# Two-layer attention kernel: paired probability-times-value matmuls and a zero-padded sink matmul

## The chip, the cores and the metric

The kernel runs on one core of one Trainium2 chip. The metric is the device time of one execution in microseconds; the time shown for a kernel is the median of its runs. A core has five engines that run their own instruction queues in order and meet at semaphores: TensorE (PE in the profile; its weight loads are the rows PEld), VectorE (DVE), ScalarE (ACT), GpSimd (POOL) and SyncE (SP), which issues most of the DMA loads.

## The reference

The reference computes three blocks over 512 latent tokens and 256 context tokens of 1024 features: an attention block with a window and a sink, a gated-scan block, and a second block with another attention, a state-space branch and routed experts. What matters here is the attention of the first block, for 16 heads in 4 groups that share keys and values:

```python
def softmax_with_sink(s, sink):
    sk = sink.astype(jnp.float32)[None, :, :, None, None]
    m = jnp.maximum(jnp.max(s, axis=-1, keepdims=True), sk)
    e = jnp.exp(s - m)
    return e / (jnp.sum(e, axis=-1, keepdims=True) + jnp.exp(sk - m))
...
    def attend_block(args):
        q, k, v, blk = args
        ...
        s_lat = jnp.einsum('bqhgd,bkhd->bhgqk', q, k).astype(jnp.float32)
        s_lat = jnp.where(ok, s_lat, NEG_INF)
        s_ctx = jnp.einsum('bqhgd,bkhd->bhgqk', q, k_ctx).astype(jnp.float32)
        p = softmax_with_sink(jnp.concatenate([s_lat, s_ctx], axis=-1), sink_g).astype(v.dtype)
        return (jnp.einsum('bhgqk,bkhd->bqhgd', p[..., :n_loc], v)
                + jnp.einsum('bhgqk,bkhd->bqhgd', p[..., n_loc:], v_ctx))
```

A block of 128 latent queries sees the blocks of keys to its left and right, itself, and the 256 context keys; a block of context queries sees the context keys alone. The sink is one more logit for each head that has no value. The second block's attention is causal, over 8 heads of 64 features, with a table of relative biases and no sink.

## The kernel before

**Scores.** The first attention is written in `layer0_attn`. `scores(qb, j)` works for one block of 128 queries and one group of four heads. For each head it fills a score tile `S` of two PSUM banks (`bank2`, a ring of two tiles): matmuls of the query with the high and the low part of the keys (L576, L577 for the window, L582, L583 for the context), two additions of a triangular mask (L579, L581), and the sink as one more column: a matmul of `one3`, three rows of ones, with `sink3`, the sink in three bf16 parts on three rows (L584). VectorE takes the maximum (L585), ScalarE the exponential with its sum (L593), VectorE the reciprocal (L595), and GpSimd multiplies the probabilities with it (L596).

**Values.** `values(*two)` works for two groups at once, because the output of a group has 64 features and so takes a half of the array's columns. For each tile of 128 keys, a chunk, it turns the probabilities of each group's four heads with four transposes (L617) into a bank `T`, copies the bank to SBUF (ScalarE for the first group, L623; VectorE for the second, L621), and issues one value matmul for each group (L626). Both write into one bank `O`, the first on partitions 0 to 63, the second on 64 to 127. Each matmul waits for the copy of its own group's operand.

**Numbers.** There are 12 rounds, 8 over latent and 4 over context queries. Latent blocks have 4 or 5 chunks, context blocks 2, for two pairs of groups each: 44 chunks, so 44 pairs of value matmuls. There are 96 heads by blocks, and so 96 score tiles and 96 sink matmuls.

**What stands around it.** The generators of scores and values are stepped in turn, so that the values of one round are issued between the scores of the next. Among them stand twelve calls of `mod_half`, which load weights of the modulation (the tiles `raw`) and multiply with them (L348). The banks of `bank()` are a ring of four, which `T`, `O` and the modulation share.

**Order.** The kernel's instructions are put in order by a scheduler that is part of the compiler: it simulates the engines as it goes and gives each engine's queue the order in which the simulated instructions became ready. The order is then fixed; the engines do not reorder on the chip. An added dependency so changes the order of the queues around it.

**The second attention** is in `block2_mix` and has the same pattern: `values` for two heads, with four chunks of 512, 384, 256 and 128 columns, transposes at L1551, copies at L1555 (ScalarE) and L1553 (VectorE), and value matmuls at L1557; 16 pairs. Beside them stand the projections of the gates (L240, L242, L244).

Of the kernel before, what the change touches and what calls it, by code (L numbers as in the profile page):

```python
# [12 lines left out]
BF = mybir.dt.bfloat16  # L13
# [47 lines left out]
class Small:  # L61
    """One packed array of per-partition columns."""
# [85 lines left out]
class Kern:  # L148
# [30 lines left out]
    def opened(self, pool):  # L179
        """(pool, stack that closes it)"""  # L180
        st = ExitStack()
        return st.enter_context(pool), st

    def scratch(self, side="right"):
        """Opens the pool of the norms' temporaries."""
        st = ExitStack()
        self.s = st.enter_context(self.tc.tile_pool(name="scratch", bufs=1, side=side))
        return st

    def residual(self, ctx):  # L190
        """Tiles of [lat0..3, ctx0, ctx1], the ctx ones in a pool of their own."""
# [17 lines left out]
    def unit(self, ap, r=None, to=None, after=None, pool=False):  # L209
        """The parts of 2048 columns of weights; after: what ACT and DVE are to do first."""  # L210
# [18 lines left out]
    def mm3(self, out, ah, al, bh, bl, start, stop):  # L229
        """out += (ah+al)^T (bh+bl) less the al bl term's 2^-24."""  # L230
# [5 lines left out]
    def mm3s(self, outs, ah, al, bhs, bls, start, stop):  # L236
        """Several moving operands over one stationary one."""
# [7 lines left out]

    def rsqrt(self, ss, n, dim):
        """1/sqrt(ss/dim + eps), [P, n]."""
# [20 lines left out]
    def prenorm(self, x, scale, shift, h, col, wide=True, dv=0, pool=False):  # L268
        """x [P tokens, D] -> columns col.. of h^T (hi, lo [P, KC, T])."""
# [28 lines left out]
    def postnorm(self, x, y, gate, pool=True):  # L298
        """x += y/rms(y) * gate; y is [P, D] as one AP or two."""
# [34 lines left out]
    def mod_half(self, pool, l, m, half, tag="rows", raws=("raw", "raw"), own=None):  # L334
        """Columns 512 half.. of modulation vector m of layer l."""
# [27 lines left out]
    def mod_affine(self, l, which, ks=slice(0, KC)):  # L363
        """Per-feature scale and shift of the pre-norm: for lat (0) and ctx (1)."""
# [13 lines left out]
    def mod_gate(self, l, which, b, pool):  # L378
        """gate * g_post on all partitions, [P, D]."""
# [13 lines left out]
    def inproj(self, hs, unit, m, outs, kcs=KC):  # L393
        """outs[g] [P features, N tokens] = (unit column chunk m)^T h^T of token group g."""
# [7 lines left out]
    def natproj(self, h, t, units, outs, kcs=KC):  # L402
        """outs [P tokens of tile t, 256] = h unit, for each unit; h's low part comes last."""
# [11 lines left out]
    def natproj1(self, h, t, unit, out, kcs=KC):  # L415
        """out [P tokens of tile t, 256] = h unit."""
# [11 lines left out]
def first_norm(K, h):  # L428
    """Modulations 0 and 1 of layer 0 and its first pre-norm, from the inputs."""
# [3 lines left out]
    with K.left("start") as sp, K.scratch():  # L433
# [23 lines left out]
        # the first half of the features goes ahead of the second half's modulations  # L457
# [15 lines left out]
def layer0_attn(K):  # L473
    """Attention of both streams: o^T of ctx and of lat (f32 [P, KC, T]), in a pool left open on the right."""
# [10 lines left out]
    with ExitStack() as left:  # L485
# [11 lines left out]
        # sink in three bf16 parts, one to a partition  # L497
        sk = qp.tile([P, 3, 16], BF, name="sk")
        sr = qp.tile([P, 16], F32, name="sr")
        sink3 = qp.tile([3, 16], BF, name="sink3")  # L500
        one3 = qp.tile([3, P], BF, name="one3")
        nc.vector.memset(one3, 1.0)
# [53 lines left out]
        with K.right("att", 2) as ap:  # L556
            def scores(qb, j):
                """exp(scores - max) of the group's four heads and 1 / their sums."""
# [42 lines left out]
            def values(*two):  # L601
                """The outputs of two groups, which take a half of the array's columns each."""
# [3 lines left out]
                for c, kt in enumerate(tiles):  # L606
# [7 lines left out]
                    for i, (_, _, pr, _, _) in enumerate(two):  # L614
# [5 lines left out]
                        if i:  # L620
                            nc.vector.tensor_copy(ts[i], T)  # L621
                        else:
                            nc.scalar.copy(ts[i], T)  # L623
                    for i, t in enumerate(ts):
                        vs = slice((j + i) * 64, (j + i) * 64 + 64)
                        nc.tensor.matmul(O[i * 64:i * 64 + 64], V[:, kt, vs], t, start=c == 0, stop=c == nt - 1,  # L626
                                         skip_group_check=True)
# [31 lines left out]
def out_full(K, w_units, tiles, finish, side="right", pre=(), cut=KC - 1, loaded=None, halves=False):  # L659
    """Tokens by D products of a whole [1024, D] matrix with o^T (f32), tile by tile: finish(i, [bank, bank])."""  # L660
    nc = K.nc
    with K.tc.tile_pool(name="wres", bufs=1, side=K.sides[side]) as wp:
# [20 lines left out]
        for x, (i, _, _) in enumerate(tiles):  # L683
            oh, ol = now
            bs = [K.bank(), K.bank()]
            if halves and x == len(tiles) - 1:
                # the last tile's first half comes early
# [20 lines left out]
def mlp(K, l, hs, nts, finish, swap, side, split=False, filler=None):  # L708
    """relu^2 MLP over token groups hs; swap() comes after the last use of hs; finish(i, [ap, ap]) gets
# [1374 lines left out]
```

## Time and profile before

| What | Value |
|---|---|
| median of 3 runs | 2373.97 us |
| lowest and highest | 2368.01 and 2375.52 us |
| span of the profiled execution | 2364.2 us |
| TensorE busy | 95% of the span |
| VectorE, ScalarE, GpSimd busy | 55%, 41%, 12% |
| mean granted clock of TensorE | 0.973 |

The profile is of one execution. Its span runs from its first to its last instruction; the time of that same execution is not given beside it, and the runs' median lies 9.8 us above the span, which holds what comes before the first and after the last instruction. "Busy" is the time in which an engine had an instruction in work. Matmuls are pipelined: a matmul's own duration is longer than the distance to the next one's start, and what a matmul occupies is read from the starts. The granted clock is given as a share of full speed: 1.00 is 2.4 GHz and 0.50 is 1.2 GHz.

### The profile page before, as it was taken

The numbers are of one execution on the slowest core, as the hardware profiler recorded it, in microseconds if no ns is written. First come the engines' busy times: TensorE is split into PE (matmuls) and PEld (weight loads), VectorE is DVE, ScalarE is ACT, GpSimd is POOL, SyncE is SP. The second block draws the span as 40 slices with busy tenths as digits, with TensorE's granted clock in tenths as the row PEclk, the third lists the DMA queues.
The fourth block names the chain that finished last, engine by engine and source line by source line (L and its number), as shares of the span: only waits on it lengthen the run. The fifth ranks groups of instructions, "written<-read, shape, count | busy, mean of one in ns | idle before, by whom it ended". The sixth has DMA issues, their size and how long they took to land. (4 is left out here: it accounts for less than half of the span.)

```text
span 2364.2 us, 31188 instructions
## 1 busy us (share of the span) xinstructions
PE 2247.1 (95%) x12608; PEld 1807.7 (76%) x12608; DVE 1306.8 (55%) x2201; ACT 969.3 (41%) x1515; POOL 291.6 (12%) x301
## 2 busy tenths in 40 slices
PE   7999999999999999989999999999999998797996
PEld 5865556888888888889977787788789875586875
DVE  3754445435444544551584558755555855347985
ACT  5434444641122112362454542222344444435874
POOL 0024431200000000230000100000030000012332
PEclk9989999999999999989999999999999999897998
DMA  6223333111121112112244223432323333567993
GB/s 280 72 90 108 107 131 120 36 54 56 69 72 54 66 60 72 36 52 72 92 180 160 84 72 108 141 107 94 109 96 99 134 121 100 147 240 278 322 310 106
DMA packets 53746, 278.10 MB, mean 118 GB/s; under 512 B 8864, under 2 KB 13360, under 8 KB 25184
## 3 DMA queue, kind: packets, MB, share of 16 engines
q1 hardware_dynamic: 42080, 248.75, 29.9%
q0 software_dynamic: 10704, 25.68, 3.8%
q8 instruction: 100, 1.64, 0.3%
q10 hardware_dynamic: 816, 1.66, 0.2%
q14 instruction: 46, 0.38, 0.1%
HBM read 263.49 MB, written 24.08 MB: 122 GB/s over the span
## 5 line engine op out<-in xcount | busy, mean ns | idle before, releaser
L213 ACT CAST whi<-raw 128x2048 fp32r<-128x2048 f32 x106 | 202.5, 1910 | 538.1 <-PE b L244 365.7
L214 DVE TENSOR_TENSOR wlo<-raw,whi 128x2048 fp32r<-128x2048 f32 x106 | 245.3, 2315 | 279.0 <-ACT whi L213 273.1
L240 PE MATMUL b<-hl,whi 128*128 128x512 f32 (+1 forms) x736 | 283.1, 385 | 1.7 <-ACT whi L213 1.7
L242 PE MATMUL b<-hl,whi 128*128 128x512 f32 (+1 forms) x736 | 283.7, 386 | 0.6 <-DVE hl L296 0.6
L783 DVE TENSOR_TENSOR acc<-acc,b 128x512 f32<-128x512 f32 x280 | 180.7, 683 | 185.3 <-PE b L244 185.3
L244 PE MATMUL b<-hl,wlo 128*128 128x512 f32 (+1 forms) x736 | 281.8, 387 | 0.0
L240 PE MATMUL b<-whi,hid 128*128 128x512 f32 x640 | 215.8, 396 | 1.8 <-DVE acc L783 1.8
L242 PE MATMUL b<-wlo,hid 128*128 128x512 f32 x640 | 217.2, 395 | 0.1
L244 PE MATMUL b<-whi,hid 128*128 128x512 f32 x640 | 214.5, 396 | 0.0
L240 PEld LDWEIGHTS b<-hl,whi 128*128 128x128 f32 x736 | 139.1, 189 | 31.3 <-ACT whi L213 2.5
L244 PEld LDWEIGHTS b<-hl,wlo 128*128 128x128 f32 x736 | 139.0, 189 | 29.5 <-issue 1.2
L242 PEld LDWEIGHTS b<-hl,whi 128*128 128x128 f32 x736 | 139.1, 189 | 29.1 <-issue 1.8
L1940 DVE TENSOR_TENSOR wlo<-raw,whi 128x2048 fp32r<-128x2048 f32 x57 | 130.0, 2289 | 29.2 <-ACT whi L1940 29.2
L242 PEld LDWEIGHTS b<-wlo,hid 128*128 128x128 f32 x640 | 120.5, 189 | 28.3 <-DVE wlo L214 0.5
L244 PEld LDWEIGHTS b<-whi,hid 128*128 128x128 f32 x640 | 120.7, 189 | 28.0
L240 PEld LDWEIGHTS b<-whi,hid 128*128 128x128 f32 x640 | 119.8, 189 | 28.5 <-DVE acc L783 2.2
L596 POOL TENSOR_TENSOR p<-p,t 128x512 f32<-128x512 f32 (+2 forms) x96 | 91.9, 968 | 234.7 <-DVE t L595 138.3
L1940 ACT CAST whi<-raw 128x2048 fp32r<-128x2048 f32 x57 | 108.3, 1911 | 10.5 <-PE b L234 10.5
L232 PE MATMUL b<-whi,hl 128*128 128x256 f32 x320 | 91.3, 285 | 2.3 <-ACT qr L1448 2.3
L233 PE MATMUL b<-wlo,hl 128*128 128x256 f32 x320 | 91.5, 286 | 0.0
L234 PE MATMUL b<-whi,hl 128*128 128x256 f32 x320 | 91.1, 285 | 0.0
L585 DVE TENSOR_REDUCE t<-b 128x1 f32<-128x513 f32 (+2 forms) x96 | 61.4, 644 | 52.1 <-PE b L584 50.9
(607 smaller groups left out, 4780.2 us busy)
## 6 DMA issues: line engine op xcount, KB each, us to landing
raw<-in_w_e_dram SPq DMA_DIRECT2D x57, 1024.0 KB, 7.2
raw<-in_w_mod_dram SPq DMA_DIRECT2D x48, 1024.0 KB, 5.0
raw<-in_w_mlp_in_dram SPq DMA_DIRECT2D x32, 1024.0 KB, 4.8
raw<-in_w_mlp_out_dram SPq DMA_DIRECT2D x32, 1024.0 KB, 4.8
raw<-in_w_in_dram SPq DMA_DIRECT2D x16, 1024.0 KB, 4.9
raw<-in_gla_in_dram SPq DMA_DIRECT2D x12, 1024.0 KB, 4.8
raw<-in_w_o_dram SPq DMA_DIRECT2D x8, 1024.0 KB, 5.0
raw<-in_w_qkv_dram SPq DMA_DIRECT2D x6, 1024.0 KB, 10.8
```

The costliest lines, as they stand in the source:

```text
L213: ins = self.nc.scalar.copy(hi, r).ins
L214: ins = ins, (self.nc.gpsimd if pool else self.nc.vector).tensor_sub(lo, r, hi.bitcast(F32)).ins
L232: mm(out, ah, bh, start=start, stop=False)
L233: mm(out, ah, bl, start=False, stop=False)
L234: mm(out, al, bh, start=False, stop=stop)
L240: mm(o, ah, b, start=start, stop=False)
L242: mm(o, ah, b, start=False, stop=False)
L244: mm(o, al, b, start=False, stop=stop)
L585: nc.vector.reduce_max(nmx[:, g:g + 1], S[:, a0:a0 + n], axis=AX.X, negate=True)
L596: nc.gpsimd.tensor_mul(p[:, :n - 1], p[:, :n - 1], den[:, g:g + 1].to_broadcast([P, n - 1]))
L783: nc.vector.tensor_add(a, a, bs[n])
L1940: ins = K.nc.scalar.copy(hi, r).ins, K.nc.vector.tensor_sub(lo, r, hi.bitcast(F32)).ins
```

## The change

The value matmuls keep their operands. A new function adds a dependency: the first matmul of a pair also waits for the copy that was issued last, which is the second group's operand on VectorE. Since both operands are then there for both matmuls, the scheduler finds them ready together. The sink's two operands get 128 partitions in place of three, with zeros in 125 of them. (The changed file also has its comments and descriptions blanked, and so line numbers move by 6 to 8: L617 is now L625, L621 and L623 are L628, L626 is L632, L584 is L592, L1551 is L1558, L1557 is L1562.)

```diff
+    def together(self, two, copied):
+        self.tc.add_manual_dep(two[0], copied.name, mybir.DependencyInfo(mybir.DependencyClass.Sync,
+                                                                         mybir.DependencyReason.DATA),
+                               reason="side by side")
...
-        sink3 = qp.tile([3, 16], BF, name="sink3")
-        one3 = qp.tile([3, P], BF, name="one3")
-        nc.vector.memset(one3, 1.0)
+        sink3 = qp.tile([P, 16], BF, name="sink3")
+        one3 = qp.tile([P, P], BF, name="one3")
+        nc.vector.memset(sink3, 0.0)
+        nc.vector.memset(one3, 0.0)
+        nc.vector.memset(one3[0:3], 1.0)
...
-                        if i:
-                            nc.vector.tensor_copy(ts[i], T)
-                        else:
-                            nc.scalar.copy(ts[i], T)
+                        copied = (nc.vector.tensor_copy if i else nc.scalar.copy)(ts[i], T).ins
+                    both = []
                     for i, t in enumerate(ts):
                         vs = slice((j + i) * 64, (j + i) * 64 + 64)
-                        nc.tensor.matmul(O[i * 64:i * 64 + 64], V[:, kt, vs], t, start=c == 0, stop=c == nt - 1,
-                                         skip_group_check=True)
+                        both.append(nc.tensor.matmul(O[i * 64:i * 64 + 64], V[:, kt, vs], t, start=c == 0,
+                                                     stop=c == nt - 1, skip_group_check=True).ins)
+                    K.together(both, copied)
...
-                        if i:
-                            v.tensor_copy(pt[:, i, d], T[:, d])
-                        else:
-                            nc.scalar.copy(pt[:, i, d], T[:, d])
+                        copied = (v.tensor_copy if i else nc.scalar.copy)(pt[:, i, d], T[:, d]).ins
+                    both = []
                     for i, (h, _, _) in enumerate(two):
-                        nc.tensor.matmul(O[64 * i:64 * i + 64, d], V[:, kt, h * 64:h * 64 + 64], pt[:, i, d],
-                                         start=kt == 0, stop=kt == 3, skip_group_check=True)
+                        both.append(nc.tensor.matmul(O[64 * i:64 * i + 64, d], V[:, kt, h * 64:h * 64 + 64],
+                                                     pt[:, i, d], start=kt == 0, stop=kt == 3,
+                                                     skip_group_check=True).ins)
+                    K.together(both, copied)
```

TensorE's queue in the first attention, kernel before, at the end of a pair of groups with five chunks. `pt` tiles hold the copied operands of two chunks, `b_2091` and `b_2126` are banks `T`, `p` are probabilities and `b_1917` is `O`:

```order
L617 MATMUL b_2091<-ident,p_1859 128x128
L617 MATMUL b_2091<-ident,p_1872 128x128
L617 MATMUL b_2091<-ident,p_1885 128x128
L617 MATMUL b_2091<-ident,p_1898 128x128
L626 MATMUL b_1917<-pt_2014,v 64x512
L617 MATMUL b_2126<-ident,p_265_1904 128x128 x3
L617 MATMUL b_2126<-ident,p_2010 128x128
L626 MATMUL b_1917<-pt_2084,v 64x512
```

The two value matmuls of a chunk stand apart, with transposes between them.

The same engine and the same groups, changed kernel (`b_1919` is `O` here; the pair of `pt_2016` has its second operand from a bank whose transposes stand just ahead of the first row shown):

```order
L632 MATMUL b_1919<-pt_1920,v 64x512 x2
L625 MATMUL b_2046<-ident,p_236_1739 128x128 x3
L625 MATMUL b_2046<-ident,p_1846 128x128
L625 MATMUL b_2052<-ident,p_1861 128x128
L625 MATMUL b_2052<-ident,p_1874 128x128
L625 MATMUL b_2052<-ident,p_1887 128x128
L625 MATMUL b_2052<-ident,p_1900 128x128
L590 MATMUL b_302_2117<-KH_428,Q_418 128x256
L591 MATMUL b_302_2117<-KL_432,Q_418 128x256
L592 LDWEIGHTS one_446
L592 MATMUL b_302_2117<-sink_445,one_446 128x1
L632 MATMUL b_1919<-pt_2016,v 64x512 x2
```

Each pair stands together (x2), and between two pairs stand the transposes of the next chunk and a score.

TensorE's queue in the second attention, last pair of heads, kernel before (`b_15346` and `b_15345` are the banks `T` of the second and the first head):

```order
L1551 MATMUL b_15346<-ident,p_16253 128x128
L1551 MATMUL b_15346<-ident,p_16294 128x128
L1551 MATMUL b_15346<-ident,p_16311 128x128
L1551 MATMUL b_15346<-ident,p_16346 128x128
L1557 MATMUL b_2356_15342<-pt_16367,v_13895 64x512
L1551 MATMUL b_15346<-ident,p_16294 128x128
L1551 MATMUL b_15346<-ident,p_16311 128x128
L1551 MATMUL b_15346<-ident,p_16346 128x128
L1557 MATMUL b_2356_15342<-pt_16380,v_13895 64x384
L1551 MATMUL b_15345<-ident,p_16220 128x128
L1557 MATMUL b_2356_15342<-pt_16380,v_13895 64x384
```

The same place, changed kernel:

```order
L1558 MATMUL b_15348<-ident,p_16255 128x128
L1558 MATMUL b_15348<-ident,p_16296 128x128
L1558 MATMUL b_15348<-ident,p_16313 128x128
L1558 MATMUL b_15348<-ident,p_16348 128x128
L1562 MATMUL b_2356_15344<-pt_16369,v_13897 64x512 x2
L1558 MATMUL b_15348<-ident,p_16296 128x128
L1558 MATMUL b_15348<-ident,p_16313 128x128
L1558 MATMUL b_15348<-ident,p_16348 128x128
L1558 MATMUL b_15347<-ident,p_16222 128x128
L1562 MATMUL b_2356_15344<-pt_16382,v_13897 64x384 x2
L1558 MATMUL b_15348<-ident,p_16313 128x128
L1558 MATMUL b_15348<-ident,p_16348 128x128
```

The first of each pair has moved down to the second, behind the second operand's transposes.

## Rows read from the trace of the kernel before

**Rows 1.** Page, first part: busy time, share of the span and instructions of each engine

```profile
PE 2247.1 (95%) x12608; PEld 1807.7 (76%) x12608; DVE 1306.8 (55%) x2201; ACT 969.3 (41%) x1515; POOL 291.6 (12%) x301
```

**Rows 2.** Windows: stretch, length, busy time of each engine, granted clock, DMA share, GB/s

```profile
130.00:392.00 262.00, 257.23 (x1568) 145.21 (x1567) 131.01 (x302) 112.20 (x260) 91.91 (x96) 0.97 0.32 112
...
1880.00:1995.00 115.00, 110.20 (x484) 75.11 (x483) 66.26 (x192) 54.54 (x113) 7.06 (x16) 0.97 0.28 96
```

**Rows 3.** TensorE's waits, 130 to 392 us: total, times, longest

```profile
PE b L576 <- ACT p L593: 1.8, 2, 1.3
```

**Rows 4.** Timeline, TensorE, first attention: start, duration, instruction, count

```profile
228.57 1.08 PE L626 MATMUL b<-pt,v 128*64 128x512 f32 x4
229.58 0.66 PE L617 MATMUL b<-ident,p 128*128 128x128 f32 x4
230.17 1.07 PE L626 MATMUL b<-pt,v 128*64 128x512 f32 x2
231.17 0.66 PE L617 MATMUL b<-ident,p 128*128 128x128 f32 x4
231.59 0.42 PE L576 MATMUL b<-KH,Q 128*128 128x384 f32 x1
...
386.24 1.93 PE L626 MATMUL b<-pt,v 128*64 128x512 f32 x6
```

**Rows 5.** Groups by line: shape, count, busy us, mean ns, idle before

```profile
L584 PE MATMUL b<-sink,one 3*128 3x1 bf16 x96 | 16.6, 173 | 0.0
```

**Rows 6.** Timeline, one score and its sink, matmuls and weight loads

```profile
211.36 0.34 PE L577 MATMUL b<-KL,Q 128*128 128x384 f32 x1
...
211.54 0.10 PEld L579 LDWEIGHTS <-identb 128*128 128x128 bf16 x1 [0.16 <-issue]
...
211.61 0.19 PEld L582 LDWEIGHTS b<-KH,Q 128*128 128x128 f32 x1
...
211.84 0.28 PE L583 MATMUL b<-KL,Q 128*128 128x256 f32 x1
...
212.04 0.09 PEld L584 LDWEIGHTS <-one 3*128 3x128 bf16 x1
...
212.15 0.14 PEld L617 LDWEIGHTS b<-ident,p 128*128 128x128 f32 x1
```

**Rows 7.** Timeline, TensorE, second attention, a 256-column matmul and its successor

```profile
1898.21 0.28 PE L1526 MATMUL b<-KL,Q 128*128 128x256 f32 x1
1898.33 0.39 PE L240 MATMUL b<-hl,whi 128*128 128x512 f32 x1
```

**Rows 8.** Timeline, TensorE: a sink, and the start of the score two later

```profile
210.98 0.17 PE L584 MATMUL b<-sink,one 3*128 3x1 bf16 x1
...
213.05 0.44 PE L576 MATMUL b<-KH,Q 128*128 128x384 f32 x1 [0.57 <-ACT p L593]
```

**Rows 9.** Lines L621 and L585, VectorE: ns min/median/max, first and last start

```profile
L621 DVE COPY pt<-b x44: 675/691/693, 164.2 to 385.7; 128x512 f32<-128x512 f32 x44
...
L585 DVE TENSOR_REDUCE t<-b x96: 408/692/827, 142.3 to 380.1; 128x1 f32<-128x513 f32 x32, 128x1 f32<-128x257 f32 x32, 128x1 f32<-128x641 f32 x32
```

**Rows 10.** Timeline, TensorE and VectorE, second attention, last pair of heads

```profile
1982.51 0.60 PE L1551 MATMUL b<-ident,p 128*128 128x128 f32 x4
1983.89 1.07 PE L1557 MATMUL b<-pt,v 128*64 128x512 f32 x2 [0.78 <-DVE pt L1553]
...
1983.15 0.69 DVE L1553 COPY pt<-b 128x512 f32<-128x512 f32 x1 [0.43 <-PE b L1551]
```

**Rows 11.** Page, DMA issues: count, KB each, median us to landing

```profile
raw<-in_w_e_dram SPq DMA_DIRECT2D x57, 1024.0 KB, 7.2
```

**Rows 12.** Windows at the start of the first attention, columns as in rows 2

```profile
145.00:148.00 3.00, 2.20 (x11) 1.73 (x11) 1.33 (x6) 2.97 (x6) 1.39 (x2) 0.80 1.03 431
148.00:151.00 3.00, 2.89 (x13) 2.11 (x13) 2.64 (x4) 1.56 (x4) 0.69 (x1) 0.50 0.26 107
```

**Rows 13.** Timeline, TensorE, the first value matmul of the stage

```profile
157.88 1.97 PE L626 MATMUL b<-pt,v 128*64 128x512 f32 x2
```

## The prediction

> **What bounds the kernel now.** The page's first part names TensorE: it works in 95% of the span [rows 1]. That is an average, so I cut the span at the two places that the change touches. From 130 to 392 us, the first layer's attention, TensorE is busy 257.23 of 262 us, VectorE 131.01, ScalarE 112.20 and GpSimd 91.91 [rows 2]. The longest reason among TensorE's waits of that stretch is 1.8 us in two times [rows 3]. So in this stage a microsecond that leaves TensorE's queue leaves the time, until another chain becomes the limit. In the second block's attention, 1880 to 1995 us, it is busy 110.20 of 115 us [rows 2], with its gaps near the end. After both stages comes work that is again TensorE's, and the loads of the expert weights are issued only as buffers come free, so an earlier start is kept.
>
> **The value matmuls of the first attention.** There are 44 pairs, 88 matmuls of 128x512, each recorded as two instructions (so x2 in the timeline is one matmul, x4 two). Each fills half of the array's columns. The timeline shows what a pair costs. Where both stand next to each other (x4) they take 228.57 to 229.58, 1.01 us; where one stands alone (x2) it takes 230.17 to 231.17, 1.00 us [rows 4]. The second half of the columns is free of charge if its matmul is next in the queue. Going through the timeline of the whole stage I count 61 entries of x2, 12 of x4 and one of x6 that lasts two units (the last row of the group): 75 units of 1.0 us. The new order has all 44 pairs adjacent, so 44 units. 31 units go, 31 us. Each unit that goes also takes its way in with it: four transposes lead to a value matmul after 0.59 us (229.58 to 230.17), while four transposes cost 0.42 where a score's matmul follows (231.17 to 231.59, [rows 4]): 0.17 us. After a sink matmul the way in costs the same as for any other work, so I take 0.1 on average, 3 us. Sum: -34 us; the ends are -31 and -36.
>
> By the Trainium skill (TensorE: Matmul & The Clock Gate, section Part 3: Packing small matmuls) a weight load overlaps a running matmul only where its group of rows differs. Both value matmuls use all 128 rows, so by that rule a pair would hold the array twice and the term would be zero. The same section gives a speed-up of 2.38 for three column tiles, which speaks for the pair. The 1.01 us of the x4 entry [rows 4] agrees with the second statement, so I go by the row.
>
> **The sink matmul.** 96 of them, 3 rows by one column, 0.17 us each [rows 5]. What one occupies is read from the starts [rows 6]: the 256-column matmul ahead of it starts at 211.84, the sink's weight load only at 212.04, the next weight load at 212.15: 0.31 us from a matmul of 256 columns to the weights of the work behind the sink. The trace of before has no 128-row matmul of one column, so it is bounded. The nearest: a 128-row bf16 weight load follows a 384-column matmul after 0.18 (211.36 to 211.54), the fp32 load behind two such bf16 ones comes 0.07 after the first of them (211.61, [rows 6]), and a 256-column matmul hands over after 0.12 elsewhere (1898.21 to 1898.33, [rows 7]). So 0.20 becomes about 0.12 and 0.11 about 0.06: 0.13 us saved, 96 x 0.13 = 12.5 us. The upper end is that only the 0.12 is left, 0.19 x 96 = 18 us; the lower end is that nothing overlaps better and the load itself takes L579's 0.10 where the 3-row one takes 0.09 [rows 6], +1 us. I take -12.5, since the mask matmul's load is the nearest in type and shape. Three memsets take the place of one on VectorE, far ahead of the first score, beside TensorE's projections; I price them at nothing. Were they late, the first sink matmul would wait for them, once, by no more than one copy of 128x512 takes, 0.69 us [rows 9].
>
> By the Trainium skill (TensorEngine Tiling (Array Packing), section Key Properties) a change of the tiling mode drains TensorE. The 0.20 us ahead of the 3-row load agrees with such a drain; no run so far shows the padded form.
>
> **What becomes late in its place.** First the ring of two score tiles: a score's tile is free when VectorE has taken its maximum and ScalarE its exponential. In the trace the sink of one score starts at 210.98 and the score two later could start only at 213.05, after a wait of 0.57 for the exponential [rows 8]: 2.07 us. Walking the order with row durations I find 13 places before, and 18 now, where the work between is shorter than that, by about 0.8 us on average. The old ones cost about 9 us in idle time and in the half clock that follows; the new ones add 5 x 0.8, and the shorter sink steps make the old ones longer by about 0.1: +5 us. Second, the added wait. The first of a pair now stands where the second stood, and with it the transposes and scores that are queued behind it on TensorE. The copy that it waits for takes 0.69 us on VectorE, behind, as a rule, no more than one maximum of up to 0.83 [rows 9]. Between the last transpose of the second operand and the pair I count mostly 1.5 to 2.9 us of other work (3 to 4 us before), because the transposes of the next chunk stand between. The first fence of the changed order shows it. So most are covered; for about a dozen near 1.5 I take 0.25 each, +3 us. If the cover were gone a pair would wait about 0.9 (rivals). Third, the last two pairs of the stage have nothing in front: +1.5 us. Sum of the stage: -34 - 12.5 + 5 + 3 + 1.5 = -37 us.
>
> **The second block's attention.** 16 pairs of 512, 384, 256 and 128 columns. In the timeline six run as pairs and ten apart: all four of 512, three of 384, two of 256, one of 128. The new order makes 15 adjacent; one of 256 keeps a score between its halves. With the 1.0 us of 512 columns and in proportion 0.75, 0.5 and 0.25 for the others that is at most 4 x 1.0 + 3 x 0.75 + 0.5 + 0.25 = 7 us. Against it stands the wait. In the last group four transposes at 1982.51, the copy at 1983.15 and the matmul at 1983.89 after 0.78 idle show what an uncovered copy costs [rows 10]; the last order fence shows the 512 pair directly behind those transposes again, and now the 384 and 128 pairs too: about 0.8 + 0.5. From 1955 to 1985 VectorE's chain sets the pace anyway, so the gain of the pairs there (one of 512, one of 384) is mostly lost. I take -4 us; ends 0 and -7.
>
> **SP and the rest.** Behind the two stages the order differs by transposes and matmuls that change places with each other, with nothing added. On SP one load of expert weights moves behind a register load that waits for the routing. It is one of 57 [rows 11], and the buffers ahead of it are filled by then: nothing; if that buffer were the next one needed, at most one landing, 7.2 us [rows 11].
>
> **Sum.** -37 - 4 = -41 us. The profiled execution's span of 2364.2 becomes 2323. The runs' median, 2373.97, lies 9.8 us above that span; I carry this over: 2333 us. From the ends: -36 - 18 - 7 with no stalls gives 2313; -31 + 1, twice the stalls (19) and nothing in the second block give 2363, but I hold all of these together for unlikely.
>
> **Rivals.**
> 1. The wait eats it: VectorE's copies come late, because it serves its queue in order, and 44 pairs wait 0.9 us each, +37 instead of +3. Then about -7 us, 2367. For it: the cover shrank by more than a microsecond nearly everywhere. Against: VectorE is busy half the time.
> 2. A pair holds the array twice when its halves belong to one output. Then only the sink's term is left, less the stalls: 2374 - 12.5 + 5, 2366. Against: the x4 rows. (The first statement of the Trainium skill's page above would be this case.)
> 3. Slower: the clock. From 148 to 151 us the granted clock is 0.50, 1.2 GHz, after stalls that left TensorE busy 2.20 of the 3 us ahead of them [rows 12]. Work at the lower level costs about twice (the x2 entry there lasts 1.97, [rows 13]). If the new, closer stalls bring that level on for more than some 45 us of work, the whole gain is gone; at 60 us it is +19, 2393. For it: fewer filler matmuls between scores. Against: the whole stage was idle for under 5 of 262 us [rows 2], and behind the start no single wait was over 1.3 us [rows 3].
> That the sink's term fails alone (2346) lies inside the forecast's range.
>
> **How the numbers follow.** The forecast with its own range, 2313 to 2357, has 0.83; rivals 1 and 2 have 0.08 and 0.04, and rival 3 has 0.05. 0.3%, 7 us, is what a measurement of this kernel can tell from no change. Rivals 1 and 2 sit at that edge: 0.06 of their 0.12 is "same". So faster 0.89, same 0.06, slower 0.05. The range 2313 to 2357 leaves out rivals 1 to 3, 17 in 100.
>
> **What would show it.** In the new trace: 44 entries of the value matmuls of about 1.05 us in the first stage; the weight load behind a sink 0.2 us, not 0.31, after the start of the matmul ahead of it; the stage some 37 us shorter, with TensorE's idle time at 10 to 15 us, named after the exponential and the value copies. Wrong would be: copies named in TensorE's waits with over 20 us, a clock of 0.5 in many slices, or a pair of over 1.5 us.

## The result, and the profile after

| | before | after |
|---|---|---|
| median of the runs | 2374.74 us (4 runs) | 2316.07 us (4 runs) |
| lowest and highest | 2368.01 and 2377.64 us | 2311.33 and 2321.64 us |
| span of the profiled execution | 2364.2 us | 2315.5 us |
| first attention | 248.0 us | 200.5 us |
| second attention | 137.6 us | 133.5 us |

The ratio of the times is 0.976, with a 95% interval from 0.9737 to 0.9784: faster, by 58.7 us where 41 were forecast. The predicted 2333 us is 17 too high. The range, 2313 to 2357, held by 3 us at its lower end; a second set of runs of the changed kernel (e5 below, 2311.44 us) lies 2 us under it.

The stages are cut here from the first score to the first cast of the stage's output (`oh`), and in the second attention from the first score to the first gate's activation. The spans differ by 48.7 us: 47.5 in the first attention, 4.1 in the second, and 2.9 given back in all the rest, which differs by a few microseconds from run to run anyway. The medians differ by 10 us more. In the runs with a known span the time lies some 2.0 us above it, not 9.8 (2317.49 over 2315.5 in the profiled execution of after), so the first profiled execution of before took some 2366 us, 8 below the median of its kernel. A second profile (e12 below), of an execution of 2376.0 us, has its additional microseconds behind the two attentions.

Windows of the two stages, kernel before (stretch, length, busy time of TensorE, its weight loads, VectorE, ScalarE, GpSimd, granted clock, DMA share, GB/s):

```profile
140.30:388.30 248.00, 244.42 (x1499) 134.41 (x1497) 123.78 (x293) 106.48 (x254) 91.91 (x96) 0.97 0.33 115
...
1857.40:1995.00 137.60, 132.80 (x585) 93.91 (x585) 85.34 (x262) 66.03 (x131) 9.46 (x21) 0.98 0.31 106
```

The same windows, kernel after:

```profile
142.10:342.60 200.50, 190.06 (x1499) 123.83 (x1497) 124.51 (x293) 105.47 (x255) 91.71 (x96) 0.97 0.39 142
...
1809.80:1943.30 133.50, 127.35 (x584) 94.11 (x583) 85.24 (x261) 66.18 (x131) 9.25 (x21) 0.95 0.31 109
```

TensorE runs as many instructions in the first attention as before, in 54.4 us less; VectorE, ScalarE and GpSimd are as busy as before. Its idle time grew from 3.6 to 10.4 us, so 47.5 of the 54.4 reach the stage's end. Over the whole kernel its busy share is still 95% (page, first part, kernel after; before in [rows 1]):

```profile
PE 2189.1 (95%) x12608; PEld 1795.7 (78%) x12608; DVE 1307.3 (56%) x2203; ACT 968.4 (42%) x1515; POOL 284.2 (12%) x301
```

A value pair and a score's end, timeline of after (compare [rows 4] and [rows 6]):

```profile
199.73 1.08 PE L632 MATMUL b<-pt,v 128*64 128x512 f32 x4
200.74 0.61 PE L625 MATMUL b<-ident,p 128*128 128x128 f32 x2
...
212.07 0.28 PE L591 MATMUL b<-KL,Q 128*128 128x256 f32 x1
212.19 0.10 PEld L592 LDWEIGHTS <-one 128*128 128x128 bf16 x1
212.20 0.18 PE L592 MATMUL b<-sink,one 128*128 128x1 bf16 x1
212.20 0.20 PEld L584 LDWEIGHTS b<-KH,Q 128*128 128x128 f32 x1
```

The pair takes 1.01 us. The sink's load starts 0.12 us after the start of the matmul ahead of it, and the next weights come 0.13 after that same start, where it was 0.31.

The groups by line of the first attention (count, busy us, mean ns, idle before and what ended it), kernel before:

```profile
L626 PE MATMUL b<-pt,v 128*64 128x512 f32 x176 | 81.2, 623 | 0.0
...
L617 PE MATMUL b<-ident,p 128*128 128x128 f32 x352 | 63.2, 290 | 1.4 <-POOL p L596 1.3
...
L348 PE MATMUL b<-raw,csil 128*32 128x256 f32 x378 | 32.3, 388 | 0.0
```

Kernel after:

```profile
L625 PE MATMUL b<-ident,p 128*128 128x128 f32 x352 | 55.0, 283 | 2.9 <-POOL p L604 2.6
L632 PE MATMUL b<-pt,v 128*64 128x512 f32 x176 | 47.9, 627 | 2.7 <-DVE pt L628 2.7
L354 PE MATMUL b<-raw,csil 128*32 128x256 f32 x378 | 23.9, 388 | 2.0 <-DVE t L603 2.0
```

The count and the mean of a matmul hardly change; the busy time falls because more of them run at the same time. That goes for the value matmuls, and also for the modulation's (L348, now L354), of which the prediction's sum says nothing. A modulation matmul takes a quarter of the array's columns (128*32 in the row). The timeline shows what it costs apart, kernel before:

```profile
220.55 0.62 PE L348 MATMUL b<-raw,csil 128*32 128x256 f32 x2
221.10 0.33 PE L617 MATMUL b<-ident,p 128*128 128x128 f32 x1
221.36 0.62 PE L348 MATMUL b<-raw,csil 128*32 128x256 f32 x2
221.91 0.33 PE L617 MATMUL b<-ident,p 128*128 128x128 f32 x1
```

and together, kernel after:

```profile
178.23 1.93 PE L354 MATMUL b<-raw,csil 128*32 128x256 f32 x32
180.09 0.39 PE L590 MATMUL b<-KH,Q 128*128 128x256 f32 x1
```

One alone holds TensorE for 0.55 us (220.55 to 221.10), sixteen in a row for 1.86. In TensorE's order of before the modulation's work of the stage stands in 29 pieces, among them such of one, two and three matmuls; in the changed order in 13, ten of them of sixteen.

To split the stage by kind of work I took each TensorE entry of the timeline from its start to the next entry's start, less the idle time marked there, and counted time at the granted clock of 0.5 by half. The "step to the sink" is that of the 256-column matmul ahead of it. The stage's last entry has no successor there and is not in the sums: three value matmuls in 1.93 us in before, e1 and e9 (the last of [rows 4]), one pair in 1.08 in the others. For the kernel before, the one after, and the experiments that answer to it, in us:

| kernel | value matmuls | modulation | step to the sink, and sink | transposes (L617) | rest | sum | idle (windows) |
|---|---|---|---|---|---|---|---|
| before | 73.3 | 29.9 | 29.7 | 44.7 | 58.7 | 236.3 | 3.6 |
| after | 43.1 | 22.5 | 17.5 | 41.6 | 58.4 | 183.1 | 10.4 |
| sink alone (e1) | 73.4 | 30.0 | 18.2 | 44.1 | 58.3 | 224.0 | 5.1 |
| pairs alone (e2) | 43.2 | 22.5 | 29.3 | 41.4 | 59.0 | 195.4 | 7.8 |
| modulation whole (e9) | 69.3 | 23.6 | 29.6 | 43.5 | 59.5 | 225.5 | 2.6 |
| modulation cut (e10) | 43.4 | 27.6 | 18.4 | 40.4 | 59.2 | 189.0 | 12.3 |

TensorE's waits of the stage after (total, times, longest):

```profile
PE b L632 <- DVE pt L628: 2.7, 4, 0.9
PE b L625 <- POOL p L604: 2.6, 4, 1.1
PE b L584 <- ACT p L601: 2.6, 3, 1.4
PE b L354 <- DVE t L603: 2.0, 1, 2.0
```

The added wait, on the second copy, ends last in four cases and costs 2.7 us. The granted clock, in windows of after:

```profile
148.00:151.00 3.00, 1.92 (x14) 1.60 (x13) 2.58 (x5) 2.95 (x7) 1.84 (x2) 0.78 0.81 336
151.00:154.00 3.00, 2.90 (x14) 2.28 (x14) 2.48 (x7) 0.91 (x4) 1.66 (x2) 0.50 0.33 89
300.00:303.00 3.00, 3.00 (x16) 0.58 (x9) 0.12 (x1) 0.00 (x0) 1.42 (x2) 0.50 0.35 79
```

It falls to 1.2 GHz at the start of the stage, as before [rows 12], and once more at 300 us, behind the wait of 2.0. Windows of 1 us add up to 13.7 us at that level in this stage, as many as before.

### The profile page after: what moved, and what is told of

Read it like the earlier page. It is cut to its first block, busy times and chain, and to the rows that moved or that the text cites. A ratio compares the mean times of both kernels' runs of the same rounds, so it can differ in the third digit from the quotient of the medians.

```text
span 2315.5 us, 31205 instructions
## 1 busy us (share of the span) xinstructions
PE 2189.1 (95%) x12608; PEld 1795.7 (78%) x12608; DVE 1307.3 (56%) x2203; ACT 968.4 (42%) x1515; POOL 284.2 (12%) x301
## 5 line engine op out<-in xcount | busy, mean ns | idle before, releaser
L240 PEld LDWEIGHTS b<-hl,whi 128*128 128x128 f32 x736 | 138.9, 189 | 30.2 <-ACT whi L213 1.3
L601 ACT ACTIVATE p<-b,t 128x513 f32<-128x513 f32 (+2 forms) x96 | 62.4, 654 | 49.9 <-DVE t L593 49.5
## 6 DMA issues: line engine op xcount, KB each, us to landing
raw<-in_w_qkv_dram SPq DMA_DIRECT2D x6, 1024.0 KB, 17.5
```

Of the source, the lines that this page charges most:

```text
L240: mm(o, ah, b, start=start, stop=False)
L601: nc.scalar.activation(p[:, :n], S[:, a0:a0 + n], AF.Exp, bias=nmx[:, g:g + 1], accum_out=den[:, g:g + 1])
```

## The experiments

In each run before was timed on the same chip; its median was 2371.49 us in e1 to e4, 2373.76 in e5 to e8, and 2372.01 in e9 to e11; e12 is a single execution. Stage lengths are of the profiled executions.

**e1 and e2: each part alone.** e1 leaves the new function out:

```diff
-                    K.together(both, copied)
+                    pass
```

> The kernel before with the sink's two operands padded to 128 rows, and no pairing; TensorE's order is that of before. My theory: from the 256-column matmul to the weights behind the sink 0.16 us in place of 0.31, as in the changed kernel's trace, so 96 x 0.15 = 14 us less, of which the stage's waits give back 1 to 3: 11 to 14 us faster, ratio 0.994 to 0.995. Rival: the gain of the sink shows only beside the pairs, because before them TensorE would wait for the exponential just as long: 0 to 4 us.

e2 keeps the pairs and takes the sink back to three rows:

```diff
-        sink3 = qp.tile([P, 16], BF, name="sink3")
-        one3 = qp.tile([P, P], BF, name="one3")
+        sink3 = qp.tile([3, 16], BF, name="sink3")
+        one3 = qp.tile([3, P], BF, name="one3")
```

> Both pairings, with the sink on three rows as before. My theory: the rest of the change, 48.7 us between the two profiled spans less 14 for the sink: 33 to 38 us faster, with 44 entries of 1.08 us for the value matmuls of the first attention. Rival, that sink and pair cover for each other (the sum of both alone is more than both together by over 5 us): 40 us or more.

e1: 2356.31 us, ratio 0.9937 (0.9913 to 0.996), 15.2 us less than before, a little more than the 11 to 14 expected; first attention 235.1 us, 12.9 less. e2: 2318.05 us, ratio 0.9768 (0.974 to 0.9796), 53.4 us less where 33 to 38 were expected, a miss; first attention 213.7, 34.3 less; second 132.7, 4.9 less. 12.9 and 34.3 make 47.2, and both together gave 47.5: in the stage the parts add up. The medians seemed to say otherwise (15.2 and 53.4 make 68.6, and e2 is only 2 us above the whole change); e5 and e8 settle that for the sink. Windows of the stage, e1 and then e2:

```profile
141.40:376.50 235.10, 230.01 (x1499) 130.44 (x1497) 123.39 (x293) 105.74 (x255) 91.91 (x96) 0.98 0.34 122
```

```profile
140.50:354.20 213.70, 205.91 (x1499) 129.94 (x1497) 124.03 (x293) 106.92 (x255) 91.68 (x96) 0.95 0.36 134
```

The clock, 0.98 and 0.95, tells why busy times must not be compared as they stand: e2 had 20.5 us at the lower level, e1 10.2. With that counted by half, the pairs took 40.9 us of work off (236.3 to 195.4; 41.7 with the last entries) and the sink 12.3 (236.3 to 224.0). The modulation's part goes with the pairs: 22.5 us in e2, 30.0 in e1.

**e3: the sink on 32 rows.** Is it the number of rows that costs, or that the array is used in another arrangement? The changed kernel with

```diff
-        sink3 = qp.tile([P, 16], BF, name="sink3")
-        one3 = qp.tile([P, P], BF, name="one3")
+        sink3 = qp.tile([32, 16], BF, name="sink3")
+        one3 = qp.tile([32, P], BF, name="one3")
```

> The changed kernel with the sink padded to 32 rows in place of 128; TensorE's order is unchanged. My theory: what costs time is that a matmul on fewer than 128 rows is another arrangement of the array, which waits for the matmul ahead to leave and is waited for, so 32 rows cost as much as 3: hand-over again 0.20 and 0.11 us, 14 us slower than the changed kernel, 2330 where that has 2316. Rival: it is the odd three rows that are slow to load; then 32 rows are as fast as 128, 2316.

2325.39 us (2330 expected; 9.3 above the changed kernel's first median, 14.0 above e5's), ratio 0.9793 (0.9761 to 0.9825); first attention 211.0 us, 10.5 more than after. Timeline:

```profile
171.22 0.28 PE L591 MATMUL b<-KL,Q 128*128 128x256 f32 x1
171.43 0.09 PEld L592 LDWEIGHTS <-one 32*128 32x128 bf16 x1
...
171.53 0.42 PEld L625 LDWEIGHTS b<-ident,p 128*128 128x128 f32 x4
```

0.31 us from the matmul to the weights behind the sink, as with three rows [rows 6]. Thirty-two rows gain nothing; of the three heights that were run only the full one does. By the Trainium skill (TensorEngine Tiling (Array Packing), section Key Properties) a change of the tiling mode drains TensorE. The 0.31 us of both small forms and the 0.13 of the full one agree with it.

**e4: both matmuls of a pair on one half of the columns.** In every chunk after a block's first,

```diff
-                        both.append(nc.tensor.matmul(O[i * 64:i * 64 + 64], V[:, kt, vs], t, start=c == 0,
+                        both.append(nc.tensor.matmul(O[:64] if c else O[i * 64:i * 64 + 64], V[:, kt, vs], t, start=c == 0,
```

> The changed kernel, but in the first attention the second value matmul of a pair writes to the same half of the columns as the first, in all chunks but the first of a block (32 of 44 pairs), so part of the output is not computed. The pairs still stand together. My theory: the gain is that two halves of the columns run at the same time; then these pairs take 2.0 us in place of 1.0, 32 us slower than the changed kernel, about 2348. Rival: the gain comes from the order (fewer changes between full and half width, no transposes between the halves); then the time stays within 8 us of the changed kernel.

2337.63 us, ratio 0.9844 (0.9811 to 0.9876), 21.6 above the changed kernel where 32 were expected; first attention 221.6 us, 21.1 more than after. Such a pair, and what follows it:

```profile
203.95 1.93 PE L632 MATMUL b<-pt,v 128*64 128x512 f32 x4
205.81 0.44 PE L625 MATMUL b<-ident,p 128*128 128x128 f32 x2
```

1.86 us in place of 1.01. 32 of the 44 pairs are of this kind, 32 x 0.85 = 27 us of work, of which less idle time (10.4 in after, 7.3 here) and less time at the lower clock (13.7 and 10.2) take some back. So standing next to each other gains nothing in itself; the different halves do. A half of the columns is here also a half of the output's partitions; e4 changes both at once and does not tell them apart. Both matmuls of a pair use all 128 rows, and in different halves they take 1.01 us together. So the Trainium skill's statement (TensorE: Matmul & The Clock Gate, Part 3: Packing small matmuls) that a load overlaps running matmuls only where its group of rows differs does not hold here. By the span that the same section of the Trainium skill gives for packed tiles, the time of one matmul and some 4 ns for each further tile, a pair would take about 1.00 us (an estimate), and the 1.01 agrees.

**e5 and e8: the whole change and the pairs alone, on one chip.**

> The changed kernel again, beside the kernel with the pairs alone on the same chip. My theory: the two parts of the change add up, because the first attention's length fell by 12.9 us with the sink alone, by 34.3 with the pairs alone and by 47.5 with both. So this kernel's first attention (first score to the first cast of its output) is again 200 to 201.5 us, and its time lies 10 to 16 us under that of the pairs alone. The rival reads the medians of the first runs (2316 here, 2318 for the pairs alone): with the pairs the sink's gain is hidden, and the times differ by under 4 us.

> The pairs alone, with the sink on three rows, beside the whole change on the same chip. My theory: the first attention takes 213 to 215 us, the time lies 10 to 16 us above that of the whole change. The rival: the sink's gain is hidden behind the pairs, and the times differ by under 4 us.

e5: 2311.44 us (2306.13 to 2313.97, 6 runs), ratio 0.9734 (0.9708 to 0.9761), first attention 197.1 us. e8: 2324.69 us (2321.31 to 2326.25, 6 runs), ratio 0.9793 (0.9768 to 0.9818), first attention 210.2. The times are 13.3 us apart, the stages 13.1: the sink's gain comes on top of the pairs', and the 2 us between the first medians, which were not timed beside each other, were scatter. The 197.1 us lie below the band that I had given (200 to 201.5), and the 210.2 below theirs (213 to 215). In e5 the wait of 2.0 us before L354 and the lower clock behind it at 300 us are gone: 10.2 us at 1.2 GHz in the stage where the first profile of the same kernel had 13.7. So one stage of one kernel varies by some 3 us.

**e6: the copies' engines exchanged.**

```diff
-                        copied = (nc.vector.tensor_copy if i else nc.scalar.copy)(ts[i], T).ins
+                        copied = (nc.scalar.copy if i else nc.vector.tensor_copy)(ts[i], T).ins
```

and in the second attention in the same way.

> The engines of the two copies change places: VectorE copies the first operand of each pair, ScalarE the second; the pairs stand together as before. My theory: the added wait is nearly covered (TensorE's waits on the second copy are 6.6 us in 10 times in the first attention), so the engine that makes this copy matters little: the stage stays within 4 us of 200.5, and the time within 7 us of the changed kernel's. The rival: what is left of idle time in the stage comes from VectorE's queue, which takes a maximum ahead of the copy; then the waits on the second copy fall to under 2 us and the stage is 5 to 7 us shorter. The other way round, if ScalarE's exponentials ahead of the copy are longer than VectorE's maxima, these waits grow to over 12 us and the stage is over 206.

2307.51 us (2298.51 to 2310.5), ratio 0.9722 (0.9695 to 0.9749); first attention 196.3 us, 0.8 less than e5. The line of the wait in the stage:

```profile
PE b L632 <- ACT pt L628: 1.4, 2, 0.7
```

3.1 us in five times (e5) became 1.4 in two, but 3.8 in place of 2.3 are waited for GpSimd. Half of the wait goes, another takes most of its place, and the stage stays nearly as long: the added wait is not what bounds it. Against the 200.5 us of the first profile the stage is 4.2 shorter, just outside the 4 expected; against e5, which ran beside it, the theory holds. (The 6.6 us of the expectation count the waits of the weight loads and those for the first copy too; TensorE's matmuls waited 2.7 us for the second.) The 4 us between the medians are less than 0.3% of the time and not told from none.

**e7: no sink matmul.**

```diff
-                n = nl + NCTX + 1
+                n = nl + NCTX
...
-                    nc.tensor.matmul(S[:, 512 + NCTX:513 + NCTX], one3, sink3[:, h:h + 1], start=True, stop=True)
```

> The sink's matmul and its column are left out, so the sink's term is missing from the softmax. My theory: in 128 rows the sink costs only the step from one matmul to the next, 0.16 us in the place of 0.12 without it, so TensorE's busy time in the first attention falls by 96 x 0.04 = 4 us, the stage is 3 to 5 us shorter, the time 2 to 8 us less than the changed kernel's. The rival: a sink of 128 rows still holds the array for about as long as it is recorded, 0.17 us, so without it the stage is 12 to 16 us shorter.

2308.68 us, ratio 0.9729 (0.9703 to 0.9755), 2.8 us less than e5; first attention 194.1 us, 3.0 less. The sum of TensorE's work is 178.0 us in the split of the table above, against 183.3 in e5: 0.055 us for each sink. So of the 0.18 us in the padded sink's row two thirds lie beside other work. The rival is out. Without a sink the next work starts 0.13 us after the 256-column matmul:

```profile
148.25 0.28 PE L591 MATMUL b<-KL,Q 128*128 128x256 f32 x1
148.38 0.33 PE L625 MATMUL b<-ident,p 128*128 128x128 f32 x1
```

**e9: the modulation in whole pieces, without the pairs.** The kernel before, with one line's condition and place changed:

```diff
-                        if n == 1 and (x > 8 or i == 0) and mods:
+                        if n == 2 and (x > 8 or i == 0) and mods:
```

> The kernel before (no pairs, sink on three rows), but each modulation half is issued one score later, behind the third head. In its order the modulation's matmuls of the first attention, which take a quarter of the array's columns each, then stand in 15 pieces in place of 29 as before and 13 in the changed kernel; of the value matmuls 70 entries stay apart in place of 74 to 75. A new theory: besides the value pairs the change also brought the modulation's quarters together, and that is the part of the gain that my sum lacked (with the half clock's time taken out, modulation entries hold TensorE for 29.9 us before and 22.5 after). Then this kernel's modulation entries hold TensorE for 23 to 24.5 us, its value entries for 68 to 70 (73.3 before), and its first attention has 9 to 13 us less TensorE work than before (5 to 13 shorter with its stalls). The rival: the missing gain lies in the way in to the value matmuls, and the modulation's pieces only share out work differently; then 3 to 5 us less, from the value entries alone.

2354.12 us, ratio 0.993 (0.9905 to 0.9956); first attention 236.1 us, 11.9 less than before. Groups by line:

```profile
L626 PE MATMUL b<-pt,v 128*64 128x512 f32 x176 | 76.9, 623 | 0.0
...
L348 PE MATMUL b<-raw,csil 128*32 128x256 f32 x378 | 24.6, 383 | 0.0
```

The modulation's row falls from 32.3 to 24.6 us, in the split from 29.9 to 23.6, and the value matmuls', with 70 entries in place of 74, from 73.3 to 69.3: the new theory's numbers. The whole is 10.8 us less work, from a line that only issues the same instructions later.

**e10: the pairs together, the modulation cut.** The changed kernel, with the modulation issued one score earlier and ahead of the values' step:

```diff
+                        if n == 0 and (x > 8 or i == 0) and mods:
+                            K.mod_half(ap, *mods.pop(0))
                         if n != 1:
                             next(last, None)
-                        if n == 1 and (x > 8 or i == 0) and mods:
-                            K.mod_half(ap, *mods.pop(0))
```

> The changed kernel, but each modulation half is issued one score earlier: all 44 value pairs stand together, and the modulation's matmuls stand in 27 pieces in place of 13. The new theory, priced from entries of the traces (0.46 us for every four matmuls begun, 0.1 for the piece): 8 more steps of four and 14 more pieces, 5 us more TensorE work in the first attention than in the changed kernel, of which 22.5 us become 27 to 28.5 for the modulation; the stage is 3 to 9 us longer, as the stalls move. The rival: pieces cost nothing, the modulation's work stays within 1 us of 22.5.

2316.28 us, ratio 0.9761 (0.9739 to 0.9783), 4.8 above e5 on another chip, which by itself tells little; first attention 205.3 us, 8.2 more than e5 and 4.8 more than after. Groups by line:

```profile
L632 PE MATMUL b<-pt,v 128*64 128x512 f32 x176 | 48.1, 624 | 6.0 <-DVE pt L628 5.3 <-DVE t L603 0.7
L354 PE MATMUL b<-raw,csil 128*32 128x256 f32 x378 | 30.4, 396 | 0.6 <-DMA raw<-in_w_mod_dram 0.5
```

The value pairs cost what they cost in after, the modulation 30.4 us in place of 23.9 (27.6 in place of 22.5 in the split, in its band). From both sides the modulation's pieces have a price of their own.

**e11: a version that goes on from e6.** One more modulation half in the first round:

```diff
-                        if n == 1 and (x > 8 or i == 0) and mods:
+                        if n == 1 and (x > 8 or x == 0 or i == 0) and mods:
```

> The version with the copies' engines exchanged, and a second modulation half moved from the end of the first attention into its first round, where TensorE waits for exponentials and for GpSimd's multiplication and then works at the lower clock for some 10 us. My theory: 1.9 us of matmuls that depend on neither fill part of these waits (two of 1.44 and 1.08 us), so TensorE's idle time in the stage falls by 1 to 3 us and, where the lower clock then stays away, the work at it by up to 5: the stage takes 189 to 196 us, the time is 0 to 7 us less than with the exchange alone. The rival: the modulation's weights are not there yet (the load queue is full at 145 to 148 us), TensorE waits for them instead, and the stage is as long or up to 4 us longer.

2308.74 us (2306.45 to 2318.77), ratio 0.9743 (0.9717 to 0.9768); first attention 192.7 us, 3.6 less than e6. Windows of the stage, e6 and then e11:

```profile
140.00:336.30 196.30, 188.10 (x1499) 122.23 (x1497) 122.33 (x293) 105.24 (x255) 92.25 (x96) 0.97 0.39 145
```

```profile
140.40:333.10 192.70, 184.00 (x1499) 119.40 (x1498) 122.32 (x293) 104.88 (x255) 92.19 (x96) 1.00 0.40 148
```

The lower clock stayed away altogether (1.00; e6 had 10.2 us of it), and that is the gain, 4.1 us of busy time. The idle time did not fall as I had expected (8.7 us, and 8.2 in e6). In the time nothing of it is to be seen. The work between the stages was 3.5 us longer than in e6, which is within what it varies (1463.5 to 1472.9 us over the profiles of e1 to e10); the second attention took 135.8 us, against 132.7 to 133.7 in the other kernels with pairs, and why was not looked for. e6 and e11 are the fastest complete versions that were run, not told apart from each other, nor e6 from the changed kernel.

**e12: the kernel before once more.** No edit; a second profile.

> The kernel before once more, for a second profile of it. The spans of the first two profiles differ by 48.7 us, the medians by 58 to 62. My theory: the two attentions take about the same time in every execution (first 246 to 251 us, second 137 to 139), and what an execution of 2374 us has more than the first profiled one of some 2366 lies in the rest of the kernel, as scatter. The rival: the first attention itself is longer in the usual execution (over 251 us, through a longer time at the lower clock), and the change is worth more in it than the 47.5 us of the first pair of profiles.

2376.0 us, span 2374.0. First attention 247.6 us (248.0 in the first profile), second 137.8 (137.6); up to the second's end the two executions differ by 0.2 us (1995.2 and 1995.0). Nearly all of the 9.8 us between the spans lies behind it. TensorE's waits there, first profile:

```profile
PE b L1393 <- DVE mT L1630: 7.6, 1, 7.6
PE b L1397 <- DMA ssm_w<-ssm_k: 4.6, 1, 4.6
...
PE b L1393 <- DMA ssm_g<-ssm_g: 1.5, 1, 1.5
```

Second profile:

```profile
PE b L1393 <- DVE mT L1630: 9.2, 1, 9.2
PE b L1397 <- DMA g<-gates_d: 7.3, 1, 7.3
...
PE b L1393 <- DMA ssm_g<-ssm_g: 3.4, 1, 3.4
```

That is the state-space branch, at the start of the stretch, with loads behind two of the three waits; together they are 6.2 us longer. The stretch from the second attention's first gate to the end took 364.0 to 378.8 us over all the profiles, in no order of the changes. So the stages' gain, 51.6 us in the first pair of profiles and 55.0 with e5's, is what the change shows. The medians differ by 58 to 62 us, and e5's interval begins at 56.7, so the scatter of this stretch may not be all of the rest. Between e12's execution and e5's, both near their kernels' medians, e5's has 3.3 us less between the stages and 5.5 less behind them; whether a part of that is the change's was not settled.

## Why the prediction was right, and what it lacked

**The bound** was right. TensorE's queue set the stage, and 47.5 of 54.4 us that left it left the stage.

**The value pairs.** 31 units of 1.0 us were forecast; the table has 30.2 (73.3 to 43.1), and with the stage's last entries it is 31.0 (75.2 to 44.2). 3 us were forecast for the way in; the transposes' column fell by 3.1 (44.7 to 41.6), but in e9 it fell by 1.2 with only four value entries and 14 modulation pieces fewer, so how much of it is the way in to the value matmuls is not shown. e4 shows that the free second half is the cause of the 31.

**The step that failed** is that only the value matmuls were taken to move. I counted their entries in the order and in the timeline, and did not count those of L348, although a modulation matmul uses a quarter of the columns and so has its price for standing alone too (0.55 us, where sixteen take 1.86). The scheduler, with the pairs tied, also put the modulation together, 29 pieces into 13: 7.4 us (29.9 to 22.5) that the sum lacked. e1 and e2 show that the tied pairs brought this, not the sink (30.0 and 22.5). That it is a cost of its own, the other two show: e9 brought 6.3 of it without a tie, e10 took 5.1 back with all pairs kept. Why the scheduler's order does so was not looked into.

**The sink.** 12.5 us were forecast, 12.2 measured (29.7 to 17.5), 11.5 in e1's column and 12.3 in its sum. I expected the next weights 0.2 us behind the start of the matmul ahead of the sink; it is 0.13 in the row above. e7 gives what is left, 5 us.

**What becomes late.** 9.5 us more waiting were forecast, 6.9 measured in the first profile of after; 4.9 in e5 (8.5 idle). The waits are those named, the exponential and the copies, with GpSimd's multiplication beside them, at 10.4 us in the band of 10 to 15.

**The second attention**: -4 forecast, -4.1 measured, -4.9 in e2. The -4 was picked between ends of 0 and -7, and no run here parts the pairs' gain from the waits, so the agreement is in part luck. One of the ten pairs counted as apart, of 128 columns, already ran together before.

**The sum.** -37 for the stage against -47.5: 7.4 from the modulation, 2.6 from fewer stalls, the rest from roundings. The other part of the miss is the offset: I carried 9.8 us from the span to the median, where 2.0 belong to an execution and 7.8 are of the size of the scatter that e12 shows. 10.5 + 7.8 and 0.1 of the second attention, less the 2.9 that the rest of the kernel gave back, make 15.5, the distance from 2333 to the profiled 2317.49. That the range held is in part luck: its lower end was made of larger value and sink terms (36 and 18 us) and no stalls, none of which came, while the modulation's 7.4 us are in none of its terms.

**The rivals.** The wait eats it: the second copies cost 2.7 us, not 37, and e6 shows that the stage doesn't hang on them. (44 waits of 0.9 are 39.6 and not 37, which would make that rival's time 2370.) A pair holds the array twice: that would be e4's 1.86 us, and it came only where both matmuls write to one half of the columns. The clock: 13.7 us at 1.2 GHz before and after, so no loss from it. It was the right thing to look at, all the same: it moves single stages by 3 us, and e11 shows 4 us in it.

## What to carry to other kernels

Where matmuls fill only a half or a quarter of the array's columns, count in the queue how many stand apart: here a half-array matmul alone cost 1.00 us and a pair 1.01, and a quarter-array matmul alone cost the 0.55 us that two or three in a row did. When a scheduler is led to put some together, list every narrow matmul in the stage, not only those that the change names: the order of the others may move too, as it did here. And take the distance from span to time from an execution that has both.

## What the hardware showed beside that

What a matmul of one column cost went by its form, not its work: three or 32 rows took 0.31 us from the matmul ahead to the weights behind, 128 rows, of which 125 hold zeros, 0.13, with the same result for the sum. Two or three quarter-column matmuls in a row held TensorE no longer than one: in before two took 0.55 us (183.46 to 184.01), three 0.57 (184.55 to 185.12) and one 0.55 (220.55 to 221.10); like a value matmul, each is recorded as two instructions. And the wait of 2.0 us at 297 us, with the lower clock behind it, came in one of two profiles of the same kernel.
